# Raw weight loads issued from GpSimd's queue instead of SP's in a two-layer hybrid backbone

## The chip, the cores and the metric

The kernel runs on one core of one Trainium2 chip. The metric is device time in microseconds (us) of one execution; a time for a kernel is the median of several runs. The engines are named as in the profile: PE is TensorE (matmuls; PEld its weight loads), DVE is VectorE, ACT is ScalarE, POOL is GpSimd and SP is SyncE, which only issues DMAs here. A name with a q behind it (SPq, ACTq) is an engine's instruction queue.

## The reference

Two layers run over 512 latent tokens and 256 context tokens of width 1024. What one layer computes, cut to its parts:

```python
h = modulate(rms_norm(x, norm1_g), shift, scale)     # adaLN: m = silu(c) @ ada_w + ada_b
proj = concat([h_ctx, h_lat]) @ w_in                 # 1024 -> 7696 columns
ya = conformer_conv(...)                             # 31-tap depthwise conv, layer norm, silu
yb = neighbourhood_attention(...)                    # 8 heads, 8x16 window plus all of the context
yc = gated_deltanet(...)                             # 4 heads, chunked, both directions
z = ga * (ya @ w_br[0]) + gb * (yb @ w_br[1]) + gc * (yc @ w_br[2])
x = x + m[2] * (z @ w_out)
h2 = modulate(rms_norm(x, norm2_g), m[3], m[4])
u = dwconv3(h2 @ ffn_up) + ffn_conv_b                # 1024 -> 5632
x = x + m[5] * ((silu(u_gate) * u_val) @ ffn_down)   # 2816 -> 1024
```

The second layer returns the latent tokens alone, so its context half is computed only as far as the latent tokens read it. All of it is float32.

## The kernel before

Activations lie transposed in SBUF, eight tiles of 128 channels by tokens, each split into a high part and a low rest in fp32r (`hl`/`ol` for latent, `hc`/`oc` for context tokens). Every product is three fp32r matmuls: high by high, high by low, low by high.

The weights are split the same way on the chip, a unit of 128 partitions by up to 1088 columns at a time. `wunit` (L146) does it: `raw` (L141) takes one of two buffers named `raw` and starts a DMA of 448 to 544 KB into it (L143); ACT copies it to `whi` (L150), DVE subtracts to make `wlo` (L151), and both have three buffers. So the load of unit i+2 can start only when `wlo` of unit i is done, and `whi` of unit i+3 only when PE is done with unit i. There are 320 such units. `ahead` (L154) and the generators that go through `fill` request the next unit while PE works on the one before.

The order of stages in a layer: gate and decay projection (`og_proj`), the delta-net projections, then `gdn_core` for two pairs of heads. Its triangular inverse (`gdn_inverse`) sends small blocks to DRAM and back, in layouts that PE can use (tiles `E`, `Eb`, `Tf`, `Tt`, `Td`; L948 to L976). While it waits, `fill` puts other projections in between (`pjl`, `pjc`, `na`), by amounts written out in the table `FILL`. Then come attention (L1054 on), with the convolution's taps on DVE, the merge (`mbl`), the output projection (`wo`), and the gated FFN (`upl`, `dn`). During the merge, the output projection and the FFN of the first layer, DVE also computes the later adaLN vectors from 256 KB tiles (`at`, L264). In layer 0, `out_proj` goes over the latent tokens and then over the context's 256; in layer 1 it goes twice over 256 latent tokens. Each pass reads all eight units of `w_o` again.

At the start SP issues, in this order: the constants, eight tiles of `x` (256 KB each), adaLN weights (`ar`, eight of 1 MB), parameters, eight tiles of the context and then the first two raw units.

The order on each engine's queue is made by the framework's planner at build time, from the order of the program as a priority and its own estimate of when an operand will be ready; `issue_after` adds an order by hand in places. On the chip each queue is worked through in that order: an instruction that waits holds all those behind it on its queue. ACT issues a few stores (`mg`, `na`, `yc`, `yb`). POOL has no DMAs before the change; it has 32 memsets, among them those of `yp` (L533 to L536), `Eb` (L946) and `TA` (L971), each with a wait for the buffer it fills. A DMA's completion is counted on one of eight semaphores in turn, and the next DMA on that semaphore is issued when the one before on it has landed.

Of the kernel before, what the change touches and what calls it, by code (L numbers as in the profile page):

```python
# [64 lines left out]
class Net:  # L65
# [74 lines left out]

    def raw(self, src, n):  # L141
        r = self.wp.tile([128, WCOL], F32, tag="raw", name="raw", bufs=2)
        self.nc.sync.dma_start(r[:, :n], src)  # L143
        return r

    def wunit(self, src, n):  # L146
# [1301 lines left out]
```

## Time and profile before

| | |
|---|---|
| median of 3 runs | 2603.09 us (2597.68 to 2608.0) |
| the profiled execution | 2592.68 us, its span 2590.9 us |
| PE busy in the span | 2495.3 us (96%) |
| DVE, ACT, POOL busy | 1853.1, 1068.0, 8.4 us |
| mean granted TensorE clock | 0.983 of full speed |

The span goes from the first to the last instruction of the program. The profiled execution was 10.4 us quicker than the median of the runs, so a sum made from its rows is carried over to the median as a difference. Busy PE includes the pipelined overlap of matmuls, so a busy share near one says that PE was never long without work, not that it ran at its peak.

### The profile page before, as it was taken

The page shows a single profiled execution, that of the slowest core. Times are in us where ns is not written, and L with a number is a line of the kernel's source. Part 1 is how long each engine was busy: PE and PEld are TensorE (multiplying, and loading weights), DVE is VectorE, ACT ScalarE, POOL GpSimd, SP SyncE. Part 2 cuts the span into 40 slices and gives each one's busy share as a digit, 9 for nine tenths or more (in the row PEclk, how much of TensorE's full clock was granted, in tenths as well). Part 3 has the DMA queues.
Part 4 walks back from the last instruction along what each step waited for, and adds up shares of the span by engine and source line. Part 5 has one row for each costly group of instructions (what it writes and reads, how often), then busy time and mean ns, then how long its engine had stood idle before and what let it go on. Part 6 is the DMA issues. An engine that isn't in the chain of part 4 may idle for free. (4 is left out here: it accounts for less than half of the span.)

```text
span 2590.9 us, 42262 instructions
## 1 busy us (share of the span) xinstructions
PE 2495.3 (96%) x16079; PEld 2154.6 (83%) x16079; DVE 1853.1 (72%) x4138; ACT 1068.0 (41%) x2158; POOL 8.4 (0%) x32
## 2 busy tenths in 40 slices
PE   6999999999999999999999999998989999999999
PEld 3989898977778888888888898888877778988887
DVE  6676578799679988876656477776768977755463
ACT  3464343445342344223223355634344543533242
POOL 0000000000000000000000000000000000000000
PEclk8999999999999999999999989998999999999999
DMA  7223524353468554453442342343446375423332
GB/s 249 90 80 121 147 88 138 104 192 108 151 187 267 184 172 127 123 158 121 142 136 90 110 139 94 122 134 111 147 124 212 99 245 191 132 90 98 98 98 89
DMA packets 207275, 356.75 MB, mean 138 GB/s; under 512 B 54832, under 2 KB 103200, under 8 KB 206944
## 3 DMA queue, kind: packets, MB, share of 16 engines
q1 hardware_dynamic: 182176, 320.97, 39.4%
q10 hardware_dynamic: 24896, 33.09, 3.6%
q8 instruction: 126, 2.06, 0.3%
q14 instruction: 77, 0.63, 0.1%
HBM read 297.31 MB, written 56.68 MB: 137 GB/s over the span
## 5 line engine op out<-in xcount | busy, mean ns | idle before, releaser
L151 DVE TENSOR_TENSOR wlo<-raw,whi 128x1024 fp32r<-128x1024 f32 (+2 forms) x320 | 387.2, 1211 | 290.4 <-ACT whi L150 287.7
L150 ACT CAST whi<-raw 128x1024 fp32r<-128x1024 f32 (+2 forms) x320 | 332.6, 1040 | 605.4 <-PE dn L169 197.3
L169 PE MATMUL upl<-hl,whi 128*128 128x512 f32 (+1 forms) x728 | 282.1, 389 | 2.2 <-ACT whi L150 2.1
L169 PE MATMUL upl<-ol,whi 128*128 128x512 f32 (+1 forms) x728 | 281.7, 388 | 0.0
L169 PE MATMUL upl<-hl,wlo 128*128 128x512 f32 (+1 forms) x728 | 280.4, 386 | 0.2 <-DVE wlo L151 0.2
L546 DVE SCALAR_TENSOR_TENSOR ca<-yp,caw,ca 128x783 f32<-128x783 f32 (+1 forms) x240 | 213.6, 890 | 8.5 <-ACT ca L539 5.6
L475 PE MATMUL pjl<-hl,whi 128*128 128x512 f32 x512 | 211.1, 412 | 7.6 <-ACT whi L150 7.6
L475 PE MATMUL pjl<-ol,whi 128*128 128x512 f32 x512 | 206.6, 403 | 0.0
L475 PE MATMUL pjl<-hl,wlo 128*128 128x512 f32 x512 | 205.8, 402 | 0.3 <-DVE wlo L151 0.2
L169 PEld LDWEIGHTS upl<-hl,whi 128*128 128x128 f32 x728 | 136.7, 188 | 30.4 <-ACT whi L150 2.3
L169 PEld LDWEIGHTS upl<-ol,whi 128*128 128x128 f32 x728 | 136.8, 188 | 29.8
L169 PEld LDWEIGHTS upl<-hl,wlo 128*128 128x128 f32 x728 | 136.7, 188 | 29.7 <-DVE wlo L151 0.4
L169 PE MATMUL dn<-fll,whi 128*128 128x512 f32 x352 | 139.1, 395 | 0.0
L169 PE MATMUL dn<-fhl,wlo 128*128 128x512 f32 x352 | 139.0, 395 | 0.0
L169 PE MATMUL dn<-fhl,whi 128*128 128x512 f32 x352 | 138.6, 395 | 0.0
L475 PEld LDWEIGHTS pjl<-hl,whi 128*128 128x128 f32 x512 | 98.1, 192 | 29.1 <-ACT whi L150 9.7
L277 DVE CUSTOM_DVE_ANT_1 aj<-at,crows,par 128x512 f32<-128x512 f32 x128 | 93.2, 749 | 31.2 <-DMA at<-ada_t 19.1
L475 PEld LDWEIGHTS pjl<-hl,wlo 128*128 128x128 f32 x512 | 97.5, 191 | 21.5 <-DVE wlo L151 1.2
L475 PEld LDWEIGHTS pjl<-ol,whi 128*128 128x128 f32 x512 | 98.0, 191 | 18.8 <-issue 0.5
L611 PE MATMUL na<-wlo,hl 128*128 128x256 f32 x384 | 108.9, 284 | 0.6 <-DVE wlo L151 0.6
L611 PE MATMUL na<-whi,hl 128*128 128x256 f32 x384 | 109.2, 285 | 0.0
L611 PE MATMUL na<-whi,ol 128*128 128x256 f32 x384 | 109.2, 284 | 0.0
(392 smaller groups left out, 6464.7 us busy)
## 6 DMA issues: line engine op xcount, KB each, us to landing
raw<-w_b SPq DMA_DIRECT2D x88, 512.0 KB
raw<-f_up SPq DMA_DIRECT2D x88, 512.0 KB
at<-ada_t SPq DMA_DIRECT2D x160, 256.0 KB
raw<-w_o SPq DMA_DIRECT2D x32, 512.0 KB
raw<-f_dn SPq DMA_DIRECT2D x32, 448.0 KB
raw<-w_a SPq DMA_DIRECT2D x24, 512.0 KB
mg<-mge ACTq DMA_DIRECT2D x48, 256.0 KB
raw<-w_br SPq DMA_DIRECT2D x24, 512.0 KB
```

Source lines behind the costliest of these rows:

```text
L150: self.nc.scalar.copy(hi[:, :n], r[:, :n])
L151: self.split = self.nc.vector.tensor_sub(lo[:, :n], r[:, :n], hi[:, :n]).ins
L169: self.nc.tensor.matmul(o, wk[a], x[k][b], start=(k == 0 and i == 0), stop=(k == n - 1 and i == 2))
L277: V.tensor_tensor_reduce(p, w, self.crows[:, r, 4 * h:4 * h + 4], 1.0, m if h else self.p(l, "adab")[:, t:t + 1], ALU.mult, ALU.add, accum ...
L475: self.nc.tensor.matmul(o, wk[a], x[k][b], start=(k == 0 and i == 0), stop=(k == n - 1 and i == 2))
L546: nc.vector.scalar_tensor_tensor(a, y[:, k:k + n], w[:, 31 * c + k:31 * c + k + 1], a, ALU.mult, ALU.add)
L611: self.nc.tensor.matmul(ps[:, :256], x[k][a], wk[b], start=(k == 0 and j == 0), stop=(k == 7 and j == 2))
```

## The change

```diff
     def raw(self, src, n):
         r = self.wp.tile([128, WCOL], F32, tag="raw", name="raw", bufs=2)
-        self.nc.sync.dma_start(r[:, :n], src)
+        self.nc.gpsimd.dma_start(r[:, :n], src)
         return r
```

All 320 loads of raw weight units are issued by POOL instead of SP. The buffers, the casts, the matmuls and all other DMAs stay where they are in the program; the planner makes its order anew.

## Rows read from the trace of the kernel before

**Rows 1.** The page, part 1: busy us (share of the span) and instructions.

```profile
PE 2495.3 (96%) x16079; PEld 2154.6 (83%) x16079; DVE 1853.1 (72%) x4138; ACT 1068.0 (41%) x2158; POOL 8.4 (0%) x32
```

**Rows 2.** Waits of SP's queue: us in total, times, longest.

```profile
SPq L143 <- DVE wlo L151: 937.4, 242, 20.8
```

**Rows 3.** Tile raw: issue ns min/median/max; then what ended ACT's waits before its casts.

```profile
L143 SPq DMA_DIRECT2D raw<-w_b x88: 327/328/1567, 57.4 to 2075.7; - x88
...
  DMA raw<-w_o: 16.9, 11
```

**Rows 4.** POOL's groups: busy us, mean ns, then idle before and its releasers.

```profile
L971 POOL MEMSET TA<- 128x768 f32 x4 | 3.0, 740 | 717.9 <-DMA tokk<-tok 284.3 <-PE oT L933 259.1 <-DMA na<-ev 174.5
```

**Rows 5.** Waits of PE, whole span.

```profile
PE nps L314 <- DVE nac L306: 19.3, 3, 11.7
PE iy L986 <- DMA Td<-e: 10.7, 5, 4.0
...
PE PT L1135 <- DVE P L1128: 7.2, 6, 4.8
```

**Rows 6.** Chain of waits, output projection of layer 1: start us, us, what.

```profile
2173.27 3.41 DMA raw<-w_o
...
2176.78 1.06 ACT whi L150
...
2177.87 0.35 DVE wlo L151
...
2179.12 3.56 DMA raw<-w_o
...
2191.75 3.52 DMA raw<-w_o
...
2217.35 4.00 DMA raw<-f_up
```

**Rows 7.** Waits in 915 to 960, end of layer 0's output projection.

```profile
ACT whi L150 <- DMA raw<-w_o: 9.5, 5, 4.1
...
PE upl L169 <- ACT whi L150: 2.1, 1, 2.1
```

**Rows 8.** Waits in 1490 to 1535, the change of layers.

```profile
ACT whi L150 <- DMA raw<-w_g: 2.7, 3, 1.0
...
PE og L179 <- ACT whi L150: 1.1, 1, 1.1
```

**Rows 9.** Timeline of the start: start us, us, engine, line, instruction, idle before.

```profile
11.65 1.87 PE L314 MATMUL nps<-kc,nac 128*128 128x1 f32 x8 [11.65 <-DVE nac L306]
...
27.01 1.22 SPq L143 DMA_DIRECT2D raw<-w_g  x2
...
47.59 1.10 ACT L150 CAST whi<-raw 128x1088 fp32r<-128x1088 f32 x1
```

**Rows 10.** Windows: length, then busy of PE, PEld, DVE, ACT, POOL; clock, DMA, GB/s.

```profile
0.00:11.65 11.65, 0.00 (x0) 0.00 (x0) 5.78 (x12) 6.54 (x10) 0.20 (x4) 1.00 0.81 264
...
1700.00:1775.00 75.00, 61.97 (x669) 55.90 (x667) 45.96 (x96) 26.28 (x48) 0.00 (x0) 0.84 0.49 146
...
836.00:936.00 100.00, 98.40 (x532) 84.15 (x532) 92.92 (x204) 29.60 (x42) 0.00 (x0) 1.00 0.63 199
...
2173.00:2223.00 50.00, 47.81 (x388) 47.42 (x388) 37.73 (x72) 24.98 (x39) 0.00 (x0) 0.97 0.64 203
```

**Rows 11.** Timeline of SP's queue, first inverse of layer 1.

```profile
1695.28 2.19 SPq L948 DMA_DIRECT2D e<-E  x4
...
1701.36 0.35 SPq L143 DMA_DIRECT2D raw<-w_b  x1
1701.89 0.69 SPq L949 DMA_DIRECT2D Eb<-e  x1
```

**Rows 12.** Timeline of SP's queue, start of layer 1's attention.

```profile
1974.57 4.75 SPq L1096 DMA_DIRECT2D vl<-na  x7
1979.37 3.26 SPq L1117 DMA_DIRECT2D bias<-bias  x3
1984.13 0.33 SPq L143 DMA_DIRECT2D raw<-w_b  x1
```

## The prediction, made before the change was run

> **What bounds the kernel now.** I read the page's busy times first, then who waits for whom on PE and on SP's queue, and then, stage by stage, the chain of waits and the windows. PE is busy for 2495.3 of 2590.9 us [rows 1]: 95.6 us without work are all that a better order of transfers could give back. A third of it is the start, where PE first runs at 11.65 us [rows 9] and waits 19.3 us in all for the norm [rows 5]. What waits for transfers directly is small: 10.7 us for the blocks of the inverse [rows 5].
>
> SP's queue looks blocked by the raw loads: they wait 937.4 us there, 242 times, for `wlo` to free their buffer [rows 2]. The reader should not take this for lost time. SP has nothing to compute; a wait there costs only if a transfer behind it was ready and its reader stood still for it. I went through SP's queue in order of time, and the transfer behind such a wait is nearly always one that becomes ready later still. The clear exception that bears on a chain is the inverse: the four stores to `e` are issued from 1695.28 on, the raw load holds the queue until 1701.36, and the load of `Eb` goes out at 1701.89, directly behind it [rows 11].
>
> The other side of the matter is where a raw load itself is on the path. Over most of the kernel a unit lands well before ACT wants it, because PE works some 5 to 8 us on one. With 256 columns per matmul, PE needs under 3 us a unit and the loop of the two buffers shows: load 3.41 us, cast 1.06, subtraction, and the next load of the same buffer starts at 2179.12, 5.85 us after the first [rows 6]. There the whole chain is made of raw loads and casts, and PE is idle for 2.19 of 50 us [rows 10].
>
> **The change part by part.** Let d be what a raw load takes longer from its buffer's release to its landing when POOL issues it. The trace has no DMA from POOL, so d is bounded. Below: SP's own issue takes 328 ns [rows 3], and if POOL did it at no cost d would be -0.33 us. Above: the longest issue of a raw load on SP is 1567 ns [rows 3], so +1.57 us. I take +0.8: the nearest row of POOL at all is its memset of 128x768, 740 ns [rows 4], and the list of a transfer over 128 partitions, made by POOL, is work of about that kind. As a rule on this, the Trainium skill's page "DMA: Bandwidth & Descriptors" (section "Latency and other measured facts") says that POOL's transfers, whose descriptors software writes, reach their first byte after about 1 us, and those of SP after about 0.6; by it d would be an estimated 0.4, the terms in d half as large, and the sum 5 us smaller.
>
> *Output projection of layer 1.* From 2173.27 to 2217.35 the raw loads hand over to each other [rows 6]: 44.08 us by links of 5.85 to 6.3 us are 7 links in each of two interleaved chains. ACT goes over to a unit as it lands, so nothing hides d: 7d = 5.6 us.
>
> *End of layer 0's output projection.* ACT waits for raw units 5 times, 9.5 us, and PE for the first FFN unit 2.1 us [rows 7]. Five waits in two interleaved chains are about 3 links: 3d = 2.4 us. The pass before it, over 512 columns, is covered: DVE is busy 92.92 of 100 us there [rows 10], and comes to `wlo` after the cast anyway.
>
> *Change of layers.* Three waits for raw units of 2.7 us in all, of which 1.1 us reach PE [rows 8]: 1d = 0.8 us. Scattered units elsewhere that land just in time, some of the 11 waits for `w_o` [rows 3] and their like in the FFN: 2d = 1.6 us. The other raw loads, nearly all of the 320, have PE's work on the units in hand as cover; that cover is gone only when d exceeds about 3 us. Sum of the terms in d: 13d = 10.4 us.
>
> *The start.* The first two raw loads stand behind all of SP's other loads, at 27.01 us, and their cast comes at 47.59 [rows 9]. On POOL nothing stands before them, so they go out in the first microsecond, beside `x`. The DMA engines are 81% busy at 264 GB/s until 11.65 [rows 10], about 326 GB/s when full; 2 x 544 KB take 3.4 us of that. The norm of `x` waits for its last tile, so PE's first matmul, and the chain behind it up to the first projection, is later by that. Bounds 0 (POOL is so late that `x` has passed) and 4.2 us (at 264 GB/s); I take 3.2.
>
> *Attention's start.* At 1984.13 a raw load goes out behind seven loads of `vl` and three of `bias` [rows 12], and it had a free buffer earlier. On POOL it overtakes them and takes 512 KB of the same engines: 1.6 us at 326 GB/s, just where PE waits longest for DVE's `P`, 4.8 us [rows 5], which needs the bias. I take 1.5 us in each layer, 3 in all; bounds 0 and 5.
>
> *The inverse.* `Eb` need not wait for the raw load. The last store to `e` is issued by 1697.47 [rows 11], and if it lands about as late as a raw load (3.41 us [rows 6]), `Eb` gains some 1 us, at most the 4.4 between 1697.47 and 1701.89, in the first inverse of each layer. Against this, raw loads that waited behind the inverse's transfers now run beside them; one flight of 3.4 us is the worst. I take -2 us in all, bounds -8.8 and +6.8.
>
> *What POOL's queue adds.* A raw load is now behind POOL's memsets where the planner puts them so. `TA`'s memset waits up to 284.3 us [rows 4], but only because nothing else is on POOL; the same buffers are waited for by the transfers that already sit beside the raw loads on SP. I cost this at nothing; its price where the planner errs is one late unit, some 3 us.
>
> *Sum:* 10.4 + 3.2 + 3 - 2 = +14.6, so +15 us: the profiled execution's 2592.68 would become 2607.7. It was 10.4 us quicker than the median of the runs; by the difference the median 2603.09 becomes 2618.
>
> **The rivals.** *No difference.* POOL's issue is as quick as SP's (d about 0.1) and the start hides its two loads: 1.3 + 0 + 3 - 2 = +2, 2605. For it: nearly all raw loads have slack, and the bytes are the same. Against it: nothing covers d from 2173 on.
>
> *Faster.* The inverse is where PE idles most after the start: 13.03 of 75 us from 1700 to 1775, at a mean clock of 0.84 [rows 10]: part of the stretch ran at 1.2 GHz, the rest at 2.4. If separate queues let the inverse's transfers through, the 10.7 us [rows 5] go, and the clock stays at its upper level around them: 0.16 of 75 us is 12 us, of which I count half, since PE also idles for other reasons there. -10.7 - 6 + 1.3 (d at 0.1) = -15, 2588. It decides from the point where the inverse's loads land 3 us earlier in all four inverses. Against it: between 1740 and 1757 SP's queue holds no raw load at all, so most of that wait is the transfers' own.
>
> *Much slower through DVE.* POOL and DVE would hold each other up: each raw issue keeps DVE for POOL's 740 ns [rows 4]. Where DVE is nearly full (92.92 of 100 us [rows 10], and attention), about 50 of the raw units are made: 37 us on top of the 15, 2655. The Trainium skill's page "SBUF — State Buffer" (section "Who interferes with whom") has DVE and POOL share one pair of ports under an exclusive lock, taken by DVE's faster modes for copies and scalar operations; nothing in this trace can show it, since POOL hardly runs. Against it: DVE's work beside the raw loads is mostly operations with two inputs.
>
> That the planner orders all queues anew is no case by itself; it may add or take a few microseconds in each, and I widen the range for it.
>
> **How the numbers follow.** Forecast (about +7 to +30, centre +15) 0.45; no difference 0.27; faster 0.15; much slower 0.13. What a measurement here can tell from no change is 0.5%, 13 us. Of the forecast's case a third lies under +13. So slower is 0.30 + 0.13 = 0.43, same 0.15 + 0.27 = 0.42, faster 0.15. The low end of all bounds, 13 x -0.33 + 0 + 0 - 8.8 = -13, is 2590; the high end, 13 x 1.57 + 4.2 + 5 + 6.8 = +36, is 2639. I set the range at 2591 to 2642, which leaves most of the fast case's lower half and most of the DVE case outside.
>
> **What would show each step.** The interval between a buffer's raw loads from 2173 on: 5.85 us now, 6.6 by the forecast, and the stretch up to the first `upl` some 5 us longer. PE's first matmul at about 15 us instead of 11.65, with the first two raw loads before 2 us. PE's wait for `P` longer by 1 to 2 us. PE's wait for `Td`: unchanged for the forecast, gone for the faster rival. DVE's mean for `wlo` of 1.21 us and for `P` longer only in the DVE rival. The prediction fails if POOL's loads land as early as SP's, or if PE's idle time in the inverses shrinks by more than 10 us.

## The result and the profile after

The changed kernel is slower: median 2669.43 us (2666.94 to 2672.59, 4 runs) beside 2600.39 us of the kernel before (2596.25 to 2608.0, 4 runs). The ratio is 1.0264, 95% interval 1.0241 to 1.0286: some 69 us more, where +15 was forecast and +42 was the upper end of the range.

The page of the changed kernel, part 1 (as [rows 1]):

```profile
span 2667.5 us, 42367 instructions
...
PE 2507.6 (94%) x16079; PEld 2161.1 (81%) x16079; DVE 1853.8 (69%) x4138; ACT 1064.5 (40%) x2158; POOL 178.8 (7%) x352
```

The span grew by 76.6 us. The instructions are the same, so PE's part of it can be read at once: PE is busy 12.3 us longer [rows 1], with a mean granted clock of 0.974 instead of 0.983, and idle 64.3 us longer (159.9 instead of 95.6). DVE's and ACT's busy times are unchanged. The loss is waiting, and some lower clock behind it.

The tile `raw`, as [rows 3]: the issue (ns min/median/max), then what ended the idle time before its readers. After it the group of `wlo` from the page (busy us, mean ns, idle time before).

```profile
L143 POOL DMA_DIRECT2D raw<-w_b x88: 527/530/680, 18.8 to 2137.5; - x88
...
  DMA raw<-w_b: 52.5, 9
```

```profile
L151 DVE TENSOR_TENSOR wlo<-raw,whi 128x1024 fp32r<-128x1024 f32 (+2 forms) x320 | 387.0, 1210 | 322.9 <-ACT whi L150 319.4 <-PE upc L169 0.4
```

The casts wait 52.5 us for loads of `w_b` alone; before, the only waits for raw loads among the longest were the 16.9 us for `w_o` [rows 3]. An issue takes 530 ns on POOL, 328 on SP [rows 3]. By the trace's issue and landing times the median raw load landed 3.54 us after the start of its issue before, and 3.81 now. `wlo` takes 1210 ns; it took 1211.

The waits of PE, whole span, as [rows 5], and after them the one for `pjl` before:

```profile
PE pjl L475 <- ACT whi L150: 20.5, 6, 9.5
PE PT L1135 <- DVE ls L1127: 18.2, 2, 10.9
PE ada L240 <- DMA ar<-ada_w: 16.5, 1, 16.5
PE iy L986 <- DMA Td<-e: 15.8, 2, 13.1
...
PE nps L314 <- DVE nac L306: 9.2, 3, 5.7
```

```profile
PE pjl L475 <- ACT whi L150: 7.6, 5, 2.6
```

The start (`ada`, now the first matmul, and `nps`) waits 25.7 us instead of 19.3. The three others are longer than before. `pjl` is the projection that fills the gaps of the inverse; it waited 7.6 us, 2.6 at most. `PT` are the transposes of attention's `P`. One wait for `Td` is 13.1 us where the longest was 4.0 [rows 5]. The windows that answer to [rows 10] (same columns): up to PE's first matmul, the first inverse of layer 1, the output projection of layer 1.

```profile
0.00:16.48 16.48, 0.00 (x0) 0.03 (x1) 6.80 (x12) 7.25 (x11) 2.45 (x8) 1.00 0.89 324
1734.30:1830.80 96.50, 79.14 (x809) 72.19 (x808) 50.58 (x105) 31.86 (x61) 5.53 (x11) 0.91 0.49 136
2243.00:2298.00 55.00, 50.84 (x398) 49.73 (x397) 38.04 (x72) 24.13 (x37) 8.36 (x16) 0.94 0.54 178
```

The inverse's stretch is 21.5 us longer, with 140 more matmuls of the fill in it, and PE is idle for 17.36 us instead of 13.03; in the output projection for 4.16 instead of 2.19. Laid side by side by the first matmul of each stage, the spans grew in the gdn cores (their inverses in them) by 41 us, in the attentions by 14, in the merges by 12, in the output projections by 9, at the start by 2. The profiled execution of before ran some 10 us under the median of its runs, and of these sums about as much is not the change's.

### The profile page after: what moved, and what is told of

Read it like the earlier page. It is cut to its first block, busy times and chain, and to the rows that moved or that the text cites. A ratio compares the mean times of both kernels' runs of the same rounds, so it can differ in the third digit from the quotient of the medians.

```text
span 2667.5 us, 42367 instructions
## 1 busy us (share of the span) xinstructions
PE 2507.6 (94%) x16079; PEld 2161.1 (81%) x16079; DVE 1853.8 (69%) x4138; ACT 1064.5 (40%) x2158; POOL 178.8 (7%) x352
## 4 chain that ended last, share of the span: by engine, by line
PE 43%; issue 11%; DMA 6%; DVE 6%; ACT 1%; POOL 1%; SPq 0%; POOLq 0%; ACTq 0%; DVEq 0%
PE upl L169 17%; PE dn L169 7%; PE upc L169 4%; PE pjl L169 2%; PE pjl L475 2%; PE wo L169 2%; PE mbl L169 1%; DVE wlo L151 1%; DMA at<-ada_t 1%; DMA raw<-w_o 1%; DVE ca L546 1%; PE og L179 1%; DMA raw<-w_b 1%; PE pjc L169 1%; PE na L611 1%
## 5 line engine op out<-in xcount | busy, mean ns | idle before, releaser
L151 DVE TENSOR_TENSOR wlo<-raw,whi 128x1024 fp32r<-128x1024 f32 (+2 forms) x320 | 387.0, 1210 | 322.9 <-ACT whi L150 319.4
L475 PEld LDWEIGHTS pjl<-hl,whi 128*128 128x128 f32 x512 | 98.1, 192 | 42.1 <-ACT whi L150 22.8
```

Of the source, the lines that this page charges most:

```text
L151: self.split = self.nc.vector.tensor_sub(lo[:, :n], r[:, :n], hi[:, :n]).ins
L475: self.nc.tensor.matmul(o, wk[a], x[k][b], start=(k == 0 and i == 0), stop=(k == n - 1 and i == 2))
```

## Experiments

The theories. **A, collisions:** before, SP's one queue kept some raw loads behind the transfers of the inverse, of the attention and of the start. From POOL they leave as soon as a buffer is free, fly beside these transfers, and both land later. **B:** every raw load is later by d. **C, order:** the planner, which writes every engine's order anew, made a worse one.

**The queue alone, the order alone.** In both programs each instruction keeps its number from tracing, so the order of one can be held in the other by edges that add no wait:

```diff
+def in_order(tc):                      # ORDER: instruction numbers, engine by engine
+    seen = {i.name: i for i in tc.nc.cur_bb.bb.instructions}
+    for names in ORDER.values():
+        for a, b in zip(names, names[1:]):
+            tc.add_manual_dep(seen[b], a, NoSync ...)
         Net(tc, A, out).run()
+        in_order(tc)
```

The first kernel is the changed one with the order of before on PE, DVE, ACT and SP (the raw loads in their old succession on POOL).

> Raw loads on POOL as in the changed kernel, but every instruction of PE, VectorE, ScalarE and SyncE held to the order that it has in the kernel before (order only, no added waits). Theory A (collisions: a raw load that SyncE's order had held back now leaves as soon as its buffer is free and flies beside the inverse's and the attention's own transfers, and both land later) needs only the queue: about 2650 to 2675 us, the wait of PE for Td in layer 1 again near 13 us. Theory C (the planner's other order of PE, VectorE and ScalarE costs the time): 2605 to 2620 us, that is the kernel before plus the start's 3 us and about 5 to 10 us for loads that land 0.3 to 0.5 us later.

Measured: 2639.99 us, ratio 1.0146 (1.0110 to 1.0183). Between the two theories: the queue alone costs 38 us, and the other 31 of the 69 came with the planner's order. The second kernel is its mirror: the kernel before, with the changed kernel's order on PE, DVE and ACT.

> Raw loads back on SyncE, but every instruction of PE, VectorE and ScalarE held to the order that it has in the changed kernel; where the raw loads stand on SyncE's queue is left to the planner. Theory A: 2600 to 2620 us, since SyncE's one queue keeps the raw loads out of the strings of other transfers again. Theory C: 2645 to 2680 us, with PE's idle time in the two gdn cores of layer 1 still near 19 us each.

Measured: 2668.0 us, ratio 1.0238 (1.0199 to 1.0276). But it is no clean measure of the order. The waits from 0 to 80 us (us in total, times, longest):

```profile
PE nps L314 <- DVE nac L306: 33.3, 2, 27.3
...
ACT whi L150 <- DMA raw<-w_g: 27.3, 1, 27.3
```

The new order has ACT cast the first raw unit early, and SP has that load behind `x`, so the start is 25 us longer. Of the 62 us by the ratio some 37 are left without it. Most of them lie in one place: the gdn cores of layer 1 (from the first `kk` to attention's first `aT`) take 330.8 us, 328.4 in the changed kernel, 309.7 in the first kernel of this section and 298.7 before. The waits of PE in the first of these two cores (1713 to 1880), and its waits for `Td` in the whole span:

```profile
PE pjl L475 <- ACT whi L150: 18.8, 2, 17.9
```

```profile
PE iy L986 <- DMA Td<-e: 12.8, 2, 11.0
```

So with the raw loads back on SP the new order has the two long waits of the changed kernel as well. It is the worse order on either queue: on POOL 69 us against the old one's 38, on SP 62 against 0.

**Which loads.** Held to the same order, the two kernels can be compared load by load. Only 15 of the 320 raw loads leave before a transfer that stood ahead of them on SP: the first two, two in each of the four inverses, two at the head of each attention, one in a merge. In the next kernel each of them waits on POOL until such a transfer has landed:

```diff
+HOLD = {423: 197, 429: 298, 4170: 3257, ...}   # raw load: transfer of SP, 15 pairs
+    for a, b in HOLD.items():
+        tc.add_manual_dep(seen[f"I-{a}"], f"I-{b}", Sync ...)
```

> The first experiment's kernel (all raw loads on POOL, every other engine in the order of the kernel before), with 15 of the 320 raw loads held: these are the ones that left before a transfer which stood ahead of them on SyncE in the kernel before, by 1 to 32 us. Each now waits on POOL until a transfer of SyncE has landed, chosen so that it leaves about when it left in the kernel before. Theory A (these few loads collide with the strings of the inverse, the attention and the start): about 2608 to 2622 us, what stays over 2603 being loads that land 0.3 us later. Theory B (the 0.3 us of every load, wherever it stands, is the cost): unchanged from that kernel, 2635 to 2650 us.

Measured: 2621.13 us, ratio 1.0061 (1.0038 to 1.0085). The complement has only these 15 on POOL:

```diff
-        self.nc.sync.dma_start(r[:, :n], src)
+        (self.nc.gpsimd if self.nraw in EARLY else self.nc.sync).dma_start(r[:, :n], src); self.nraw += 1
```

> The complement: the kernel before, in its own order on every engine, with only those 15 raw loads on POOL and the other 305 on SyncE. Theory A: 2615 to 2635 us, most of the 37 us that the first experiment's kernel lost. Theory B: 2600 to 2608 us, since 15 loads that land 0.3 us later can't cost more than 5 us.

Measured: 2623.25 us beside 2604.23, ratio 1.0061 (1.0038 to 1.0085). So neither theory has it all: the 15 loads alone cost 16 us by the ratio, and 16 are left when they are held and the other 305 leave from POOL. The two together are about the 38 of the first kernel. What the 305 cost is not yet shown to be d. The collision can be read from what the readers of `Td` wait for (tile `Td`, all engines: us, times), first where the loads overtake, then where they are held:

```profile
L975 SPq DMA_DIRECT2D Td<-e x16: 303/524/3278, 307.0 to 1931.1; - x16
...
  DMA Td<-e: 53.3, 17
```

```profile
L975 SPq DMA_DIRECT2D Td<-e x16: 303/523/762, 306.7 to 1912.6; - x16
...
  DMA Td<-e: 30.5, 18
```

Issue and landing times from the trace give the price for each inverse. The second string runs from the first store after the substitution to the last landing of a `Td` or `E` block (sums of the unrounded times). The last column is PE's idle time, in all four inverses, from the first store to `e` (L948) to the first `ir` of L1027:

```
us, inverse:              1      2      3      4     sum   PE idle
before                  19.7   19.1   18.5   21.2   78.5      30.7
all on POOL, old order  23.6   20.7   23.5   23.6   91.3      47.0
15 held                 20.2   18.5   19.1   21.0   78.8      36.1
only 15 on POOL         23.6   21.1   22.2   22.7   89.5      40.1
changed kernel          23.2   21.0   25.1   25.9   95.1      53.1
```

Where the loads overtake, the strings are 11 to 13 us longer in the old order and 17 in the changed kernel; when the loads are held, they are back to the length of before. PE's idle time goes the same way. PE's wait for `Td` in the last inverse, the changed kernel, the first kernel and the held one:

```profile
PE iy L986 <- DMA Td<-e: 13.1, 1, 13.1
```

```profile
PE iy L986 <- DMA Td<-e: 7.3, 1, 7.3
```

```profile
PE iy L986 <- DMA Td<-e: 4.4, 1, 4.4
```

The step from 4.4 to 7.3 goes with the overtaking loads. Most of the step to 13.1 is the order's: with the new order and the loads on SP this wait is 11.0.

**Term by term.** Two kernels like the one with 15 loads on POOL take a part of them, and a third takes other loads; only the list `EARLY` differs.

> The kernel before in its own order, with only the two raw loads of each of the four inverses on POOL (8 of the 15). It measures one term of the prediction by itself. Theory A: plus 7 to 13 us, 2611 to 2617 us, as the landing of Td and of the E blocks goes from 2.5 to about 4 us in each inverse and PE waits for it. The prediction's own step: 2 us less, between 8.8 less and 6.8 more.

Measured: 2615.29 us beside 2606.76, ratio 1.0043 (1.0028 to 1.0058): +11 us. The four strings took 88.8 us, 10.3 more than before, and PE was idle for 40.3 us in the inverses instead of 30.7. That is about the whole loss, but one profile tells it to some 5 us only: in the two kernels of the next experiments, where no raw load overtakes in an inverse, the strings took 79.1 and 83.0 us and PE's idle time was 32.7 and 36.6. Most of it lies in layer 0: the stretches of its two inverses, measured like the idle time, are 9.7 us longer, those of layer 1 together 1.7. Theory A's number, and outside the prediction's bounds for the inverse.

> The kernel before in its own order, with only the two raw loads at the head of each attention on POOL (4 of the 15). Theory A: plus 6 to 12 us, 2610 to 2616 us. The prediction's own step: plus 3 us, 2607 us.

Measured: 2609.22 us, ratio 1.0007 (0.9993 to 1.0021): +2 us (-2 to +5). Theory A's 6 to 12 lie outside; the prediction's 3 lies inside, and so does nothing.

> The kernel before in its own order, with only the 32 raw loads of the output projection's weight on POOL; none of the 15 is among them. It measures the two largest terms in d of the prediction by themselves: 7d + 3d were 8 us with d = 0.8; with the 0.28 us by which the loads landed later in the earlier runs and 0.2 us more for the issue, 10d is 3 to 5 us, 2606 to 2609 us beside 2603. If loads from POOL that overtake nothing cost nothing: 2603.

Measured: 2610.41 us beside 2606.23, ratio 1.0021 (1.0006 to 1.0036): +5 us.

**The order, with the loads held.** The changed kernel as it stands, the planner free, with only the 15 waits added:

> The changed kernel, its order left to the planner, with the same 15 raw loads held by the same waits, which the planner sees. If the planner's other order costs time only because it counts on these raw loads to come early: 2605 to 2630 us. If the other order is worse by itself: 2635 us or more, that is the changed kernel's 2669 less at most the 37 us that the queue alone cost.

Measured: 2638.15 us beside 2604.23, ratio 1.0093 (1.0056 to 1.0130). The interval reaches into both expectations. With 15 waits on POOL, 44 of the 69 us are taken back by the ratios (0.0171, with the two intervals combined ±0.0043), twice the 22 in the old order. But the planner sees these waits and made a third order. By the succession in the traces at least some 700 of PE's 16,079 instructions stand elsewhere than in the changed kernel and some 500 elsewhere than before. So this run doesn't tell the loads from the order; the changed kernel's own order with loads held was not run. There are also more loads to hold in it: against the succession of before, 35 raw loads leave more than 0.4 us ahead of a transfer that stood before them on SP, where in the old order there were the 15. Two places of the changed kernel's trace show what the new order does. The waits of the first gdn core of layer 1 (1702 to 1868), and the first links of its chain from 1735 on:

```profile
ACT whi L150 <- DMA raw<-w_b: 15.9, 2, 8.7
PE pjl L475 <- ACT whi L150: 15.8, 2, 9.5
```

```profile
1738.02 0.01 POOLq L143
1738.04 9.46 DMA raw<-w_b
```

The new order puts a projection into the inverse whose weights leave at 1738.04, in the middle of the inverse's transfers, and land 9.46 us later; PE stands still for them, at that place and again at 1791.87. Before, the longest such wait was 2.6 us; with the old order and all loads on POOL 6.1. On SP in the new order it was 17.9.

The second place is SP's queue in the last inverse (start us, us):

```profile
1878.11 2.42 SPq L948 DMA_DIRECT2D e<-E  x4
1889.51 0.34 SPq L516 DMA_DIRECT2D cy<-th  x1
1890.08 0.66 SPq L949 DMA_DIRECT2D Eb<-e  x1
```

```profile
SPq L516 <- DVE th L515: 8.9, 1, 8.9
```

The planner has put a store, `cy`, between the stores to `e` and the load of `Eb`. It waits 8.9 us for `th`, which waits for a projection of PE, and the inverse waits behind it: `Eb` leaves 10.1 us after the last store to `e` instead of 4.7, and `Tt`, the last of this first string, lands after 22.6 us instead of 13.9. The kernel with only the new order has the same store there (10.5 and 21.1 us). With the 15 held and the planner free, `Eb` is next on the queue and leaves after 5.6.

Attention of layer 1 has a wait of this kind for the bias (waits of DVE and of PE at its head, the changed kernel, then the kernel with only the old order):

```profile
PE PT L1135 <- DVE ls L1127: 10.9, 1, 10.9
...
DVE sc L1125 <- DMA bias<-bias: 8.1, 1, 8.1
```

```profile
DVE sc L1125 <- DMA bias<-bias: 5.5, 1, 5.5
...
PE PT L1135 <- DVE P L1128: 4.8, 1, 4.8
```

With raw loads on POOL in both, PE waits for `P` 4.8 us in the old order, as before [rows 5], and 10.9 in the new (there for `ls`, a step ahead of `P`), where it has done less fill by then: 57 matmuls from the first `aT` to the transposes instead of 96. The kernel with the new order and SP's raw loads waits 10.3 there. This wait belongs to the order, whichever queue has the loads. It is no loss by itself: by the first matmuls of the stages, layer 1's attention grew by 1.8 us in the changed kernel and by 3.5 with the old order.

**Which engine's order.** Four kernels with all raw loads on POOL and the 15 held keep the old order on some engines only.

```diff
-ORDER: PE, DVE, ACT, SP, raw loads     # the lists' names only
+ORDER: PE, raw loads     # then: DVE, ACT, SP, raw; DVE, raw; ACT, raw
```

> All raw loads on POOL, the 15 held, and only PE's instructions kept in the order of the kernel before; VectorE, ScalarE and SyncE are left to the planner. With every engine in the old order this kernel took 2621 us, with every engine left to the planner 2638. If it is PE's new order that costs the 17 us: 2615 to 2628 us. If it is that of VectorE, ScalarE or SyncE: 2631 to 2645 us.

Measured: 2654.24 us, ratio 1.0170 (1.0135 to 1.0204).

> The complement: all raw loads on POOL, the 15 held, VectorE, ScalarE and SyncE in the order of the kernel before and PE left to the planner. PE's order the cause: 2631 to 2645 us. The other engines' order the cause: 2615 to 2628 us.

Measured: 2624.2 us, ratio 1.0078 (1.0052 to 1.0104).

> All raw loads on POOL, the 15 held, and only VectorE in the order of the kernel before; the other engines left to the planner. With VectorE, ScalarE and SyncE in the old order it was 2624 us, with all left to the planner 2638. If VectorE's new order is what costs: 2618 to 2630 us; if ScalarE's: 2632 to 2645 us; above 2645 us an old order on one engine alone is worse than none, as it was for PE.

Measured: 2641.96 us beside 2598.64, ratio 1.0159 (1.0112 to 1.0206).

> The same with only ScalarE in the order of the kernel before. If ScalarE's new order is what costs: 2618 to 2630 us; if VectorE's: 2632 to 2645 us; above 2645 us an old order on one engine alone is worse than none.

Measured: 2634.38 us beside 2598.64, ratio 1.0149 (1.0101 to 1.0196).

These are inconclusive on the question. It rested on the 17 us between two medians (2621 and 2638); by the ratios that gap is 0.0032 ± 0.0044. The old order on PE alone is worse than none at all (1.0170 and 1.0093). On DVE or on ACT alone it can't be told from none: the two medians, 2642 and 2634, each fall into the range that blames the other engine. DVE, ACT and SP together do about as well as all four (1.0078 and 1.0061). SP's order alone, the one that places stores like `cy`, was not tried. No version beat the kernel before.

## Why the prediction was wrong

In the terms of the runs the 69 us are: 22 for the 15 loads that overtake (38 less 16), 16 for all others, 31 for the order that the planner made around them, each ± 6 to 11. With the loads on SP the new order cost much the same, the start aside (some 37).

*The step that failed* is the sentence "That the planner orders all queues anew is no case by itself; it may add or take a few microseconds in each". It added 31 us. The change was taken as a change of queue within a fixed order; on PE at least 771 of 14,397 instructions moved. In the profiles some 19 us of it lie in layer 1's gdn cores (309.7 us with the old order, 328.4 in the changed kernel), and two places there are shown: a projection whose weights arrive late, and a store that SP waits for ahead of `Eb`. Both are there with the loads on SP too. Why the planner puts them so, and how much would go if its order stayed and the loads were held, is open.

*The inverse* had the wrong sign: -2 was taken and +11 measured, above its bound of +6.8. This is the second step that failed. The text named the mechanism ("raw loads that waited behind the inverse's transfers now run beside them") and priced it at one flight of 3.4 us at worst, in the first inverse of each layer; and it had `Eb` gain up to 4.4 us where it waited for a raw load on SP. The gain came and was worth little: in the old order with all loads on POOL, `Eb` landed 2.3 us sooner in the first inverse of layer 0 and 2.2 in that of layer 1, but the substitution also needs `Tt`, the last load of the string, which landed 13.4 us after the last store instead of 13.3, and 14.2 instead of 15.2. The loss stood elsewhere, in the second string, and in all four inverses: 4.0, 1.8, 2.7 and 1.8 us with the 8 loads alone. There two raw loads fly beside a string of stores and loads that each wait for one another. "Between 1740 and 1757 SP's queue holds no raw load at all" was read as a sign that the wait was the transfers' own. It was the sign of what SP's order had been good for. The prediction's own sign of failing, PE's idle time in the inverses shrinking by more than 10 us, looked the wrong way: it grew from 30.7 to 53.1.

*The terms in d* were sized well. 7d + 3d were 8 us with d = 0.8; the 32 loads of `w_o` cost 5 (2 to 9). The chain of waits of layer 1's output projection, as [rows 6]:

```profile
2251.64 4.07 DMA raw<-w_o
...
2258.42 4.11 DMA raw<-w_o
...
2265.45 5.26 DMA raw<-w_o
```

The loop's interval went from 5.85 to 6.78 us and more, where 6.6 was expected, and the stretch up to the first `upl` from 50.4 to 54.5 us, where 5 us more were. The chain of the kernel with only these loads on POOL shows a part of d that the prediction had not looked for, the time between the end of `wlo` and the start of the issue:

```profile
2192.62 1.24 DVE wlo L151
2193.86 0.28 issue
2194.14 4.38 DMA raw<-w_o
```

By the traces' times it is 0.03 us in the median on SP and 0.29 on POOL. The landing, counted from the start of the issue, comes 0.27 us later. From the release of the buffer to the landing, loads that go out as soon as it is free took 3.54 us before and 4.15 in the first kernel, so d is 0.6; for `w_o` in layer 1, in the kernel with only its loads on POOL, it was 0.74 (3.58 and 4.32). The Trainium skill's figures for the first byte, about 1 and 0.6 us ("DMA: Bandwidth & Descriptors", section "Latency and other measured facts"), gave an estimated d of 0.4. That is less than was measured, and the 0.8 lay nearer; the first byte itself shows in no run. But the 305 loads that overtake nothing still cost 16 us, and the 32 of `w_o` are only 5 of it. The prediction put 2.4 us on the rest, since PE's work covers them until d exceeds some 3 us; where their some 11 us (± 7) go, one stage at a time below what a run can tell, stays open.

*The start* was right by its sign. In the old order PE's first matmul came at 14.88 us, where about 15 was expected, and in the changed kernel at 16.48. The eight loads of `x` landed in 6.46 us in the median instead of 4.02, beside the two raw loads that left at 1.3 and 1.9 us. The stretch up to the first `og` grew by 2.0 us, where 3.2 was taken; no run has these two loads alone. A smaller slip: "a third of it is the start" counts the 11.65 us twice, since the 19.3 hold them; PE was idle for 22.8 of the first 50 us, a quarter of the 95.6. *Attention's start* was not contradicted (+2 measured, -2 to +5; 3 taken). So most of the 14 us more in the attentions of the changed kernel must have other causes.

*The rivals.* DVE is not held up by POOL's issues: `wlo` 1210 ns and 1211, DVE's busy time 1853.8 and 1853.1 us. The Trainium skill's rule that DVE and POOL lock each other out of a shared pair of ports ("SBUF — State Buffer", section "Who interferes with whom") shows in no run here. This rival's 2655 us was the number nearest to the measured 2669, without its mechanism. The faster rival wanted the inverse's transfers 3 us earlier; they came later. "No difference" fell with them.

## What to carry over

A single in-order queue is also a schedule: the loads that it holds back are kept out of the way of short round trips on which an engine waits, so before moving a stream to a queue of its own, list which of its transfers will then overtake what; here 15 of 320 made about half of the 38 us that the new queue cost by itself. Where a planner writes the order, a change of queue is a change of every engine's order, and the old order, held by edges that only fix the succession, separates the two in one run. An order that a planner makes for the new queue need not be the better one there: here the old order was better on both queues, and kept on PE alone it was worse than none.

## What the runs showed of the hardware

Transfers from POOL's and SP's queues that are in flight together delay each other. With all raw loads on POOL in the old order, a `Td` block of the inverse landed in 3.8 us in the median, and in 2.5 with the 15 loads held; the longest `E` block took 11.1 and 6.9 us. A raw load beside the last inverse's blocks took 10.7 us, where the median of all raw loads was 3.8. A load from POOL is issued in 530 ns (328 on SP); its issue starts 0.29 us after the end of the instruction that frees its buffer (0.03 on SP), and it landed 0.27 us later in the median, counted from the start of its issue, than the same one from SP.
